# Attention stage rebuilt: token-major projections, head norms along rows, transposes on TensorE, output projection by chunks of its input

## The chip, the cores and the metric

The kernel runs on one core of one Trainium2 chip, as one program. The metric is the device time of one execution in microseconds. Three executions of the kernel before were timed, and one more was recorded by the hardware profiler.

## The reference, cut to what matters

The network is a trunk of two layers on 256 tokens of 1024 features, all in float32. Each layer is a gated feed-forward block (FFN), a mixer, a second FFN and a gated embedding. The mixer of layer 0 is the attention that this change rebuilds; layer 1's mixer is a pooling.

```python
x = x + 0.5 * swiglu(rms_norm(x, norm_ffn1[i]), w_ffn1_gu[i], w_ffn1_down[i])
h = rms_norm(x, norm_mix[i])
mix = stick_breaking_attention(h, w_qkv[j], q_norm[j], k_norm[j], w_o[j])   # layer 0
x = x + mix
x = x + 0.5 * swiglu(rms_norm(x, norm_ffn2[i]), w_ffn2_gu[i], w_ffn2_down[i])
gate = jax.nn.sigmoid(rms_norm(x, norm_ple[i]) @ w_ple_gate[i])
x = x + gate * (p[i] @ w_ple_proj[i])

def stick_breaking_attention(h, w_qkv, q_gain, k_gain, w_o):   # 16 heads of 64
    q, k, v = jnp.split(h @ w_qkv, 3, axis=-1)
    q = rms_norm(q.reshape(B, S, N_HEADS, HEAD_DIM), q_gain)   # a norm for each token and head
    k = rms_norm(k.reshape(B, S, N_HEADS, HEAD_DIM), k_gain)
    ...
    z = q @ k.T / 8                                            # for each head, causal
    log_stay = jnp.where(causal, jax.nn.log_sigmoid(-z), 0.0)
    log_after = lax.cumsum(log_stay, axis=3, reverse=True) - log_stay
    weights = jnp.where(causal, jnp.exp(jax.nn.log_sigmoid(z) + log_after), 0.0)
    return (weights @ v) @ w_o
```

The functions log_sigmoid and exp make ScalarE compute Abs, Exp and Ln for every score, and one more Exp for every weight.

## The kernel before, in words

**Numbers in two parts.** TensorE multiplies in fp32r. To keep float32 accuracy each operand is split into a high part (a copy rounded to fp32r) and a low part (the difference), and each product is three matmuls (`mm3`: high by high, high by low, low by high). Activations lie feature-major: 128 features on the partitions, 256 tokens along the row.

**Weights.** They stream in units of 1 MB (128 partitions by 2048 floats). `load` starts the DMA of a unit, `divide` makes its high part (line 171 on ScalarE, sometimes line 169 on VectorE) and its low part (line 173 on VectorE or GpSimd). The table `SPLIT` says for each unit into how many pieces it is cut, how many high parts VectorE makes, and how many low parts GpSimd makes. A unit not in the table is cut in two and split by ScalarE and VectorE. There are three buffers each of raw, high and low; `unit(u)` asks for the loads of units u to u+3 and for the split of u and u+1. Units 33 to 48 are the attention's, 49 is the embedding's projection, and the second FFN starts with unit 50.

**Order.** The order on TensorE and on the DMA queue is the order of the program text (`manual_schedule`). The order on ScalarE, VectorE and GpSimd is chosen by a list scheduler when the program is built; work inside `tc.high_priority()` goes ahead of other work, such as weight splits, as soon as it is ready. On the chip each engine executes its own list strictly in order.

**Attention before.** Heads are handled in eight pairs. For pair j, `heads_qk` multiplies the pair's q and k weights with the activations: 48 matmuls of 256 columns give q and k feature-major in one PSUM bank. `square_qk` squares it, twice on ScalarE, and splits the square; `norm_qk` sums the squares over the 64 features of a head by two 512-wide matmuls with a constant block matrix (`blkw`), then takes the root as Exp of -0.5 Ln, with a Newton step, on 128 by 512 elements, and writes the split q and k (lines 518 to 548). `scores` makes two score blocks (`late`: the last 128 keys by the last 128 queries, 256 wide for two heads; `all`: the first 128 keys by all queries, 512 wide), takes Abs, Exp and Ln of each (lines 566 to 568), and splits the result. `stick` adds the cumulative sums by matmuls with triangular constants, takes Exp, and splits the weights. `gather` multiplies them with the values v and splits the output `oh`, `ol`. The steps are ordered by two strings: `ITER` for one round of the loop over pairs 2 to 7 ("G Q0 N A S C Q1 X": gather of pair j-4, half of the projection, norm of pair j-1, stick of j-3, scores of j-2, the other half, squares), and `DRAIN` for the last pairs, in which pieces of the output projection (`W`) are mixed. Which of VectorE and GpSimd makes each copy and low part is set for every pair by letter tables (`SP_LOW`, `W_LOW`, `K_LOW`, `SQ_LOW` and others; "p" is GpSimd). The values are projected token-major between pairs 1 and 2. After the attention comes the layer's embedding projection (`embedding`, 48 matmuls), then the second FFN.

**Activation tables.** ScalarE holds one set of function tables at a time, and the build places an instruction ACT_TABLE_LOAD ahead of an activation whose function is not in the set that is loaded. `statistics`, the norm over all features, asks by hand for a set that holds both Ln and Exp (line 330, `preload_act_table_set`). The attention before begins with `statistics`. The pooling of layer 1 uses `token_scales` (lines 700 and 701: Ln, then Exp), which asks for no set.

Of the kernel before, what the change touches and what calls it, by code (L numbers as in the profile page):

```python
# [70 lines left out]
SP_HIGH = ("vv", "vv", "vv", "vv", "vv", "vv", "aa", "va")  # L71
SP_LOW = ("pv", "pp", "pp", "pp", "pp", "pp", "ps", "pv")
W_HIGH = ("vv", "vv", "vv", "vv", "vv", "vv", "vv", "av")
W_LOW = ("ps", "ps", "pv", "pv", "ps", "ps", "ps", "pv")

SQ_LOW = "vppvvvvv"
K_LOW = "pvvvppvv"

URGENT = ("exp", "o", "pw", "qk", "sp")

ITER = "G Q0 N A S C Q1 X"
DRAIN = (
    "W00 W03 G4 W02 N S5 C6 W01 W04 W10 W11 W12 W13 G5 "
    "S6 C7 W20 W21 G6 W14 W05 S7 W25 W06 W15 G7 W16 W23 W24"
)

@with_exitstack
def trunk(ctx: ExitStack, tc: tile.TileContext, gxT, pT, wts, outT):  # L90
# [13 lines left out]
    bufs_of = {"mm": 3, "z": 3, "st": 1, "o": 1}  # L104
# [12 lines left out]
    def next_bank():  # L117
        turn[0] += 1
        return bank("z" if turn[0] % 2 else "mm")
# [91 lines left out]
    blkw = const.tile([P, P], F32R, name="blkw")  # L211
    nc.gpsimd.memset(f(blkw), 0.0)
    for i in range(2):
        nc.gpsimd.memset(f(blkw[64 * i : 64 * i + 64, 64 * i : 64 * i + 64]), 1.0 / 64)
# [6 lines left out]
    ident = const.tile([P, P], F32R, name="ident")  # L221
    tri = const.tile([P, P], F32R, name="tri")
# [90 lines left out]
    def statistics(columns=False):  # L313
# [10 lines left out]
        if columns:  # L324
            for t in range(2):
                mm(st[:, S + t : S + t + 1], acc[:, t * P : (t + 1) * P], meanc, True, True)
# [8 lines left out]
        if not columns:  # L335
            return None
        ms = st[:, S : S + 2]
        rc = tmp.tile([P, 2], F32, tag="rc", bufs=1, name="rc")
        nc.scalar.activation(rc, ms, AF.Ln, bias=eps)
        nc.scalar.activation(rc, rc, AF.Exp, scale=-0.5)  # L340
        rsqrt_newton(rc, ms, EPS, 2, "rc")
        epsms = tmp.tile([P, S], F32, tag="epsms", bufs=1, name="epsms")
        nc.vector.tensor_scalar(
            out=epsms, in0=st[:, :S], scalar1=EPS, scalar2=EPS, op0=ALU.add, op1=ALU.mult
        )
        return rc, epsms

# [16 lines left out]
    def project_late(u, out, src, order, late):  # L364

        a, b = order[: NC - late], order[NC - late :]
        project(u, out, src, a, start=order[0], stop=order[-1])
        project(u, out, src, b, start=order[0], stop=order[-1])

    class Opening:  # L370
# [6 lines left out]
        def step(self, n=NC):  # L377
            for k in self.order[self.done :][:n]:
                for u, out in zip(self.us, self.banks):
                    project(u, out, self.src, (k,), start=self.order[0], stop=self.order[-1])  # L380
                self.done += 1

# [63 lines left out]
    def attention(u0, layer):  # L446
        uqk = [u0, u0 + 1] + [u0 + j for j in range(6, 12)]
        uv, uo = u0 + 2, u0 + 12
        with tc.tile_pool(name=name("attn"), bufs=1) as pool:
# [5 lines left out]
            gq = tmp.tile([P, 1], F32, tag="gq", bufs=1, name="gq")  # L455
            nc.vector.tensor_scalar_mul(gq, g[:, G_QK : G_QK + 1], 0.125)
            gk = g[:, G_QK + 1 : G_QK + 2]
# [8 lines left out]
            def urgent(what):  # L466
                return tc.high_priority() if what in URGENT else ExitStack()

            def copy(engine, out, v):
                if engine == "a":  # L470
                    nc.scalar.activation(out, v, AF.Copy)
                else:
                    nc.vector.tensor_copy(out, v)  # L473

            def low(engine, out, v, h, c):
                mid = (c.start + c.stop) // 2
                cuts = [c] if engine in "pv" else [slice(c.start, mid), slice(mid, c.stop)]
                for i, c in enumerate(cuts):
                    eng = nc.gpsimd if engine == "p" or engine == "s" and i else nc.vector
                    eng.tensor_sub(out[:, c], v[:, c], f(h[:, c]))  # L480

            sph, spl, wh_, wl_ = (
                pool.tile([P, S + 512], F32R, name=n) for n in ("sph", "spl", "pwh", "pwl")
            )
            qk, zs = {}, {}

            blocks = []
            for i in range(2):
                t = [pool.tile([P, 2, S], F32R, name=f"{n}{i}") for n in ("qh", "ql")]
                for v in t:  # L490
                    nc.gpsimd.memset(f(v[64:, 0]), 0.0)
                    nc.gpsimd.memset(f(v[:64, 1]), 0.0)
                blocks.append(t)

            def heads_qk(j, ps=None, halves=(0, 1)):
                ps = bank("mm") if ps is None else ps
                if j == 0:
                    project_late(uqk[j], ps, (xh, xl), list(range(NC)), 1)
                else:
                    project(uqk[j], ps, (xh, xl), halves=halves)  # L500
                return ps

            def square_qk(j, ps):
                sq = pool.tile([P, 512], F32, tag="qksq", name=name("qksq"))
                h = pool.tile([P, 512], F32R, tag="sqh", name=name("sqh"))
                lo = pool.tile([P, 512], F32R, tag="sql", name=name("sql"))
                with urgent("sq"):
                    nc.scalar.activation(h, ps, AF.Square)
                    nc.scalar.activation(sq, ps, AF.Square)
                    low(SQ_LOW[j], lo, sq, h, slice(0, 512))  # L510
                return h, lo

            def norm_qk(j, ps, sq):
                ms = bank("st")
                mm(ms, blkw, sq[0], True, False)
                mm(ms, blkw, sq[1], False, True)
                v = pool.tile([P, 512], F32, tag="qkv", name=name("qkv"))
                nc.vector.tensor_add(
                    v.rearrange("p (a b) -> p a b", a=2), ms.rearrange("p (a b) -> p a b", a=2),
                    dup(epsms),  # L520
                )
                y = pool.tile([P, 512], F32, tag="qky", name=name("qky"))
                nc.scalar.activation(y, v, AF.Ln)
                nc.scalar.activation(y, y, AF.Exp, scale=-0.5)
                t = pool.tile([P, 512], F32, tag="qkt", name=name("qkt"))
                nc.vector.tensor_mul(t, y, y)  # L526
                nc.vector.scalar_tensor_tensor(
                    out=t, in0=t, scalar=-0.5, in1=v, op0=ALU.mult, op1=ALU.mult
                )
                nc.vector.scalar_tensor_tensor(  # L530
                    out=y, in0=t, scalar=1.5, in1=y, op0=ALU.add, op1=ALU.mult
                )
                for i, gain in enumerate((gq, gk)):
                    c = slice(i * S, (i + 1) * S)
                    nc.vector.scalar_tensor_tensor(
                        out=y[:, c], in0=ps[:, c], scalar=gain, in1=y[:, c],
                        op0=ALU.mult, op1=ALU.mult,
                    )
# [3 lines left out]
                with urgent("qk"):  # L542
                    nc.scalar.activation(kh, y[:, S:], AF.Copy)
                    (nc.gpsimd if K_LOW[j] == "p" else nc.vector).tensor_sub(kl, y[:, S:], f(kh))  # L544
                    for a in range(2):
                        b = slice(64 * a, 64 * a + 64)
                        nc.scalar.activation(q[b, a], y[b, :S], AF.Copy)
                        nc.vector.tensor_sub(ql[b, a], y[b, :S], f(q[b, a]))  # L548
# [473 lines left out]
```

## Time and profile before

| | |
|---|---|
| three timed runs | 1023.67, 1023.89, 1026.84 us; median 1023.89 us |
| profiled execution | 1024.73 us, span 1023.0 us, mean granted TensorE clock 0.98 |
| TensorE (PE) busy | 982.4 us (96%) |
| VectorE (DVE) busy | 685.4 us (67%) |
| ScalarE (ACT) busy | 537.9 us (53%) |
| GpSimd (POOL) busy | 246.7 us (24%) |
| DMA | 174.79 MB, mean 171 GB/s |
| stage of attention and embedding | from 199.70 us to 361.83 us |

Times within the span are microseconds from its start. In the rows on waits, the engine ahead of the arrow waited for the one behind it. In rows grouped by line, "x18 | 17.0, 969" means 18 instructions, 17.0 us busy in all, 969 ns each in the mean. In the table by stretches each row has the stretch, its length, the busy time and the number of instructions of TensorE, its weight loads, VectorE, ScalarE and GpSimd, the granted clock, the busy share of the DMA engines and their GB/s.

### The profile page before, as it was taken

The numbers are of one execution on the slowest core, as the hardware profiler recorded it, in microseconds if no ns is written. First come the engines' busy times: TensorE is split into PE (matmuls) and PEld (weight loads), VectorE is DVE, ScalarE is ACT, GpSimd is POOL, SyncE is SP. The second block draws the span as 40 slices with busy tenths as digits, with TensorE's granted clock in tenths as the row PEclk, the third lists the DMA queues.
The fourth block names the chain that finished last, engine by engine and source line by source line (L and its number), as shares of the span: only waits on it lengthen the run. The fifth ranks groups of instructions, "written<-read, shape, count | busy, mean of one in ns | idle before, by whom it ended". The sixth has DMA issues, their size and how long they took to land.

```text
span 1023.0 us, 18925 instructions
## 1 busy us (share of the span) xinstructions
PE 982.4 (96%) x7888; PEld 963.3 (94%) x7888; DVE 685.4 (67%) x1022; ACT 537.9 (53%) x888; POOL 246.7 (24%) x293
## 2 busy tenths in 40 slices
PE   7999999998797899999999899999999999999997
PEld 7999999987687899999999899999998899999997
DVE  7956565578999857666556786565565785656574
ACT  5644444457677556454444664544346664444443
POOL 4300002865665531000051233000230200000262
PEclk9999999999898999999999899999999999999999
DMA  7655544544212246454544455555454355455531
GB/s 247 258 191 181 196 177 177 193 165 159 69 61 83 69 184 240 172 203 168 204 165 166 165 182 201 199 174 204 165 206 165 124 206 188 184 191 180 204 127 42
DMA packets 26294, 174.79 MB, mean 171 GB/s; under 512 B 2912, under 2 KB 3680, under 8 KB 5600
## 3 DMA queue, kind: packets, MB, share of 16 engines
q1 hardware_dynamic: 26208, 173.59, 47.0%
q8 instruction: 61, 1.00, 0.4%
q14 instruction: 25, 0.20, 0.1%
HBM read 172.53 MB, written 1.05 MB: 170 GB/s over the span
## 4 chain that ended last, share of the span: by engine, by line
PE 86%; DVE 10%; ACT 2%; issue 1%; DMA 0%; SPq 0%; DVEq 0%; ACTq 0%
PE mm L122 43%; PE z L122 42%; DVE wl L173 2%; DVE xx L289 2%; DVE ql L548 1%; PE o L122 1%; DVE sql L480 1%; DVE kl L544 1%; DMA gx<-gxT 0%; DVE sph L473 0%; DVE qkt L526 0%; DVE sp L570 0%; DVE ol L608 0%; DVE gx L866 0%; PE st L122 0%
## 5 line engine op out<-in xcount | busy, mean ns | idle before, releaser
L171 ACT ACTIVATE wh<-raw 128x1024 fp32r<-128x1024 f32 (+2 forms) x416 | 343.7, 857 | 312.9 <-PE z L122 126.2
L173 DVE TENSOR_TENSOR wl<-raw,wh 128x1024 fp32r<-128x1024 f32 (+2 forms) x342 | 360.5, 1072 | 105.9 <-ACT wh L171 104.9
L122 PE MATMUL mm<-xx,wh 128*128 128x256 f32 x1792 | 324.5, 282 | 0.0
L122 PE MATMUL z<-xx,wh 128*128 128x256 f32 x1536 | 277.9, 281 | 1.6 <-ACT wh L171 1.6
L122 PEld LDWEIGHTS mm<-xx,wh 128*128 128x128 f32 x1792 | 277.3, 190 | 0.5
L122 PE MATMUL mm<-xx,wl 128*128 128x256 f32 x896 | 252.4, 282 | 5.6 <-DVE wl L173 5.6
L122 PEld LDWEIGHTS z<-xx,wh 128*128 128x128 f32 x1536 | 236.7, 189 | 1.8 <-ACT wh L171 1.8
L122 PE MATMUL z<-xx,wl 128*128 128x256 f32 x768 | 216.0, 281 | 3.5 <-DVE wl L173 3.5
L122 PEld LDWEIGHTS mm<-xx,wl 128*128 128x128 f32 x896 | 170.3, 190 | 6.5 <-DVE wl L173 6.5
L122 PEld LDWEIGHTS z<-xx,wl 128*128 128x128 f32 x768 | 145.5, 190 | 4.2 <-DVE wl L173 4.1
L173 POOL TENSOR_TENSOR wl<-raw,wh 128x512 fp32r<-128x512 f32 (+1 forms) x83 | 128.0, 1561 | 84.8 <-ACT wh L171 71.6
L122 PE MATMUL z<-hx,wh 128*128 128x256 f32 x704 | 125.1, 280 | 0.0
L122 PE MATMUL mm<-hx,wh 128*128 128x256 f32 x704 | 125.1, 280 | 0.0
L293 POOL TENSOR_TENSOR acc<-gx 128x256 f32<-128x256 f32 x8 | 5.4, 670 | 486.0 <-DVE gx L441 425.3
L122 PEld LDWEIGHTS z<-hx,wh 128*128 128x128 f32 x704 | 107.5, 187 | 0.0
L122 PEld LDWEIGHTS mm<-hx,wh 128*128 128x128 f32 x704 | 107.5, 187 | 0.0
L122 PE MATMUL z<-hx,wl 128*128 128x256 f32 x352 | 98.2, 279 | 0.0
L122 PE MATMUL mm<-hx,wl 128*128 128x256 f32 x352 | 98.2, 279 | 0.0
L122 PEld LDWEIGHTS z<-hx,wl 128*128 128x128 f32 x352 | 66.1, 188 | 0.0
L122 PEld LDWEIGHTS mm<-hx,wl 128*128 128x128 f32 x352 | 66.1, 188 | 0.0
L288 ACT ACTIVATE xx<-gx 128x256 fp32r<-128x256 f32 x64 | 31.2, 504 | 66.3 <-DVE gx L441 52.7
L397 DVE TENSOR_TENSOR s<-mm,r 128x256 f32<-128x256 f32 x44 | 18.6, 422 | 57.3 <-PE mm L122 57.3
(221 smaller groups left out, 1072.0 us busy)
## 6 DMA issues: line engine op xcount, KB each, us to landing
raw<-wts SPq DMA_DIRECT2D x161, 1024.0 KB, 4.8
raw<-wts SPq DMA_DIRECT2D x7, 256.0 KB, 5.7
gx<-gxT SPq DMA_DIRECT2D x3, 256.0 KB, 5.5
outT<-gx SPq DMA_DIRECT2D x3, 256.0 KB, 2.6
p<-pT SPq DMA_DIRECT2D x2, 256.0 KB, 2.9
raw<-wts SPq DMA_DIRECT2D x2, 128.0 KB, 2.9
outT<-gx SPq DMA_DIRECT2D x2, 128.0 KB, 1.9
gx<-gxT SPq DMA_DIRECT2D x1, 165.0 KB, 2.4
```

Source lines behind the costliest of these rows:

```text
L122: nc.tensor.matmul(out, lhsT, rhs, start=start, stop=stop, skip_group_check=True)
L171: nc.scalar.activation(h[:, c], raw[u][:, c], AF.Copy)
L173: eng.tensor_sub(lo[:, c], raw[u][:, c], f(h[:, c]))
L288: nc.scalar.activation(xh[:, d], x[:, d], AF.Copy, scale=gc)
L289: nc.vector.scalar_tensor_tensor(out=xl[:, d], in0=x[:, d], scalar=gc, in1=f(xh[:, d]), op0=ALU.mult, op1=ALU.subtract)
L293: nc.gpsimd.tensor_mul(acc, x[:, d], x[:, d])
L397: nc.vector.tensor_mul(s, ps[:, :S], r)
L480: eng.tensor_sub(out[:, c], v[:, c], f(h[:, c]))
L544: (nc.gpsimd if K_LOW[j] == "p" else nc.vector).tensor_sub(kl, y[:, S:], f(kh))
L548: nc.vector.tensor_sub(ql[b, a], y[b, :S], f(q[b, a]))
```

## The change

- Q, k and v are all projected token-major (128 tokens on the partitions, 512 features along the row, that is 8 heads): six groups q0, k0, v0, q1, k1, v1, each of 8 steps of 6 matmuls of 512 columns. The weights are laid out accordingly.
- The norms of q and k are taken along rows for eight heads at once (`normalize`): a square on ScalarE, a row sum on VectorE, Ln, Exp and the Newton step on 128 by 16 elements, and a multiplication on VectorE. The matmuls with `blkw` go away.
- `transpose` turns q and k of a pair feature-major by four TensorE transposes of 128 by 128 into the one PSUM bank `st`; the gains and the scale 1/8 are applied to k in the copies.
- The order is one string, `HEADS`. The output projection `W` takes one 128-feature chunk of its input at a time and adds to all eight output tiles (four banks), so that they are all complete with W7; the residual additions follow. The embedding projection (`E`, on bank `st`) is moved ahead of the output projection.
- GpSimd makes no low parts there: units 33 to 55 are cut in four, high parts on ScalarE, low parts on VectorE, and the letter tables go away.
- The attention calls `token_scales` in place of `statistics`; the former sets no table. PSUM banks become 4 `mm` and 2 `z` (before 3 and 3).

```diff
-    32: (2, 0, 2), 34: (4, 0, 4), 35: (4, 0, 4), 36: (2, 0, 1), 37: (4, 1, 2), 38: (2, 0, 2),
-    41: (4, 0, 4), 42: (4, 0, 3), 43: (4, 0, 3), 44: (4, 0, 4), 45: (4, 0, 3), 46: (4, 0, 3),
+    32: (2, 0, 2), 33: (4, 0, 0), 34: (4, 0, 0), 35: (4, 0, 0), 36: (4, 0, 0), 37: (4, 0, 0),
+    38: (4, 0, 0), 39: (4, 0, 0), 40: (4, 0, 0), 41: (4, 0, 0), 42: (4, 0, 0), 43: (4, 0, 0),
...
-ITER = "G Q0 N A S C Q1 X"
-DRAIN = (...)
+HEADS = """
+q00 q01 q02 q03 q04 q05 N q06 q07 k00 k01 k02 k03 k04 k05 k06 k07
+v00 v01 v02 v03 T0 v04 v05 C0 v06 v07 q10 q11 S0 T1 q12 q13 C1 G0 q14 q15 q16 q17
+S1 T2 k10 k11 C2 G1 k12 k13 k14 k15 S2 T3 k16 k17 C3 G2 v10 v11 v12 v13 S3 T4 v14 v15 C4 G3
+v16 v17 E0 E1 S4 T5 W0 E2 C5 G4 E3 W1 S5 T6 W2 C6 G5 W3 W4 S6 T7 W5 C7 G6 W6 S7 G7 W7
+"""
-    bufs_of = {"mm": 3, "z": 3, "st": 1, "o": 1}
+    bufs_of = {"mm": 4, "z": 2, "st": 1, "o": 1}
+    def project_tokens(u0, ps, chunks):
+        for k in chunks:
+            wh, wl = unit(u0 + k // 4)
+            w = slice(k % 4 * 512, k % 4 * 512 + 512)
+            for t in range(2):
+                c = slice(t * P, (t + 1) * P)
+                mm(ps[t], xh[:, k, c], wh[:, w], k == 0, False)
+                mm(ps[t], xh[:, k, c], wl[:, w], False, False)
+                mm(ps[t], xl[:, k, c], wh[:, w], False, k == NC - 1)
+    def token_scales():
...
+        with tc.high_priority():
+            nc.scalar.activation(rc, st[:, :2], AF.Ln, bias=eps)
+            nc.scalar.activation(rc, rc, AF.Exp, scale=-0.5)
+            nc.vector.tensor_scalar(out=epsms, ...)
+            rsqrt_newton(rc, st[:, :2], EPS, 2, "rc")
+        return rc, epsms
+            def normalize(what, ps, epsms):
...
+                with tc.high_priority():
+                    for t in range(2):
+                        nc.scalar.activation(sq, ps[t]..., AF.Square)
+                        nc.vector.reduce_sum(out=ms[:, t], in_=sq, axis=mybir.AxisListType.X)
+                        nc.vector.tensor_scalar(out=ms[:, t], ...)
+                    nc.scalar.activation(r_, m, AF.Ln)
+                    nc.scalar.activation(r_, r_, AF.Exp, scale=-0.5)
+                    rsqrt_newton(r_, m, 0.0, 16, "rs")
+                    for t in range(2):
+                        nc.vector.tensor_mul(y[:, t]..., ps[t]..., rs[:, t]...)
+            def transpose(j):
+                st = bank("st")
+                for i, what in enumerate("qk"):
+                    for t in range(2):
+                        nc.tensor.transpose(st[:, o : o + P], normed[what, j // 4][:, t, c], identity)
...
+                    nc.scalar.activation(kh, st[:, S:], AF.Copy, scale=gk)
+                    nc.vector.scalar_tensor_tensor(out=kl, in0=st[:, S:], scalar=gk, in1=f(kh), ...)
                     for a in range(2):
+                        nc.scalar.activation(q[b, a], st[b, :S], AF.Copy)
+                        nc.vector.tensor_sub(ql[b, a], st[b, :S], f(q[b, a]))
             def scores(j):
...
+                    with tc.high_priority():
                         nc.scalar.activation(e, z, AF.Abs)
                         nc.scalar.activation(e, e, AF.Exp, scale=-1.0)
                         nc.scalar.activation(e, e, AF.Ln, bias=1.0)
...
+                        nc.vector.tensor_copy(sph[:, c], sp[:, c])
+                        nc.vector.tensor_sub(spl[:, c], sp[:, c], f(sph[:, c]))
+            def w_o(k):
+                wh, wl = unit(uo + k // 2)
+                if k == 0:
+                    ob.extend(bank("mm") for _ in range(4))
+                for m in range(NC):
+                    mm3(ob[m // 2]..., (wh[:, c], wl[:, c]), (oh[:, k], ol[:, k]), ...)
...
-            rc, epsms = statistics(columns=True)
+                elif what == "N":
+                    rc, epsms = token_scales()
```

More of the change, by code (lines that the diff above doesn't have):

```diff
@@ L210, in trunk @@
     nc.vector.memset(meanc, 1.0 / D)
[L211 to L214, printed above, removed]
     warm = bank("o")
@@ L311, in rsqrt_newton, with statistics @@
         nc.vector.tensor_mul(y, y, t)
-    def statistics(columns=False):
+    def statistics():
         nonlocal r
@@ L334, in statistics @@
             rsqrt_newton(r, st[:, :S], EPS, S, "r")
[L335 to L346, printed above, removed]
     def project(u, out, src, order=range(NC), halves=(0, 1), start=None, stop=None):
@@ L443, in ffn, with attention @@
         return u0 + UNITS_FFN
-    def attention(u0, layer):
-        uqk = [u0, u0 + 1] + [u0 + j for j in range(6, 12)]
-        uv, uo = u0 + 2, u0 + 12
+    def attention(u0, layer, embedding):
+        ue, uo = u0 + 12, u0 + 13
         with tc.tile_pool(name=name("attn"), bufs=1) as pool:
@@ L464, in pair @@
                 return t[:, c].rearrange("p (a b) -> p a b", b=n)
[L466 to L483, printed above, removed]
+            sph, spl, wh_, wl_, sp, w = (
+                pool.tile([P, S + 512], F32R if n[-1] in "hl" else F32, name=n)
+                for n in ("sph", "spl", "pwh", "pwl", "spv", "pwv")
             )
-            qk, zs = {}, {}
             blocks = []
@@ L503, in square_qk @@
[L503 to L538, printed above, removed]
@@ L539, in norm_qk @@
+            def transpose(j):
+                st = bank("st")
+                c = slice(j % 4 * P, j % 4 * P + P)
+                for i, what in enumerate("qk"):
+                    for t in range(2):
+                        o = (2 * i + t) * P
+                        nc.tensor.transpose(
+                            st[:, o : o + P], normed[what, j // 4][:, t, c], identity
+                        )
                 q, ql = blocks[j % 2]
@@ L563, in scores @@
                     zs[j].append((z, keys))
-                    e = pool.tile([P, 2, keys[1]], F32, tag=f"e{kt}", name=name("e"))
-                    with urgent("e"):
+                    e = pair(sp, keys)
+                    c = keys[0]
+                    with tc.high_priority():
                         nc.scalar.activation(e, z, AF.Abs)
@@ L568, in scores @@
                         nc.scalar.activation(e, e, AF.Ln, bias=1.0)
-                    with urgent("sp"):
                         nc.vector.scalar_tensor_tensor(
-                            out=pair(sp, keys), in0=z, scalar=0.0, in1=e, op0=ALU.max, op1=ALU.add
+                            out=e, in0=z, scalar=0.0, in1=e, op0=ALU.max, op1=ALU.add
                         )
-                        copy(SP_HIGH[j][1 - kt], sph[:, keys[0]], sp[:, keys[0]])
-                    with urgent("spl"):
-                        low(SP_LOW[j][1 - kt], spl, sp, sph, keys[0])
+                        nc.vector.tensor_copy(sph[:, c], sp[:, c])
+                        nc.vector.tensor_sub(spl[:, c], sp[:, c], f(sph[:, c]))
             def stick(j):
-                w = pool.tile([P, S + 512], F32, tag="w", name=name("w"))
                 (zl, _), (za, _) = zs[j]
@@ L638, in attention @@
-            ahead()
-            ps = ps1
-            for j in range(2, NPAIR):
-                nxt = bank("mm")
-                for step in ITER.split():
-                    if step[0] == "Q":
-                        heads_qk(j, nxt, (int(step[1]),))
-                    elif step == "G" and j >= 4:
-                        gather(j - 4)
-                    elif step == "S" and j >= 3:
-                        stick(j - 3)
-                    elif step == "N":
-                        norm_qk(j - 1, ps, sq)
-                    elif step == "C":
-                        scores(j - 2)
-                    elif step == "X":
-                        sq_next = square_qk(j, nxt)
-                    elif step == "A":
-                        ahead()
-                ps, sq = nxt, sq_next
@@ new lines, in attention @@
+            banks, rc, epsms = [], None, None
+            for step in HEADS.split():
+                what, n = step[0], step[1:]
+                if what in "qkv":
+                    group = "qkv".index(what) + 3 * int(n[0])
+                    k = int(n[1])
+                    if k == 0:
+                        banks = [bank("mm"), bank("mm")]
+                    project_tokens(u0 + 2 * group, banks, (k,))
+                    if k == NC - 1 and what == "v":
+                        c = slice(int(n[0]) * 512, int(n[0]) * 512 + 512)
+                        keep_tokens(vh[:, :, c], vl[:, :, c], banks, rc)
+                    elif k == NC - 1:
+                        normalize((what, int(n[0])), banks, epsms)
+                elif what == "N":
+                    rc, epsms = token_scales()
+                elif what == "E":
+                    embedding(int(n), tag="st")
@@ L675, in attention @@
                 else:
-                    {"G": gather, "S": stick, "C": scores}[step[0]](*n)
+                    {"T": transpose, "C": scores, "S": stick, "G": gather, "W": w_o}[what](int(n))
             begin_norm()
-            def residual(u, halves):
-                for d, ps in zip((2 * u, 2 * u + 1), halves):
-                    nc.vector.tensor_add(x[:, d], x[:, d], ps)
-                    norm_chunk(2, layer, d, d == 0, sqs=("mixer", 0))
-            for u in range(3):
-                w_o(u, *[k for k in range(NC) if k not in done[u]])
-                residual(u, (ob[u][:, :S], ob[u][:, S:]))
@@ L687, in attention @@
-            last = [bank("z"), bank("z")]
-            project(uo + 3, last, src)
-            residual(3, [t[:, :S] for t in last])
-        return u0 + 16
-    def token_scales():
-        st = bank("st")
-        for t in range(2):
-            mm(st[:, t : t + 1], acc[:, t * P : (t + 1) * P], meanc, True, True)
-        rc = tmp.tile([P, 2], F32, tag="rc", bufs=1, name=name("rc"))
-        with tc.high_priority():
-            nc.scalar.activation(rc, st[:, :2], AF.Ln, bias=eps)
-            nc.scalar.activation(rc, rc, AF.Exp, scale=-0.5)
-            rsqrt_newton(rc, st[:, :2], EPS, 2, "rc")
-        return rc
+            for d in range(NC):
+                with tc.high_priority():
+                    nc.vector.tensor_add(
+                        x[:, d], x[:, d], ob[d // 2][:, (d % 2) * S : (d % 2 + 1) * S]
+                    )
+                    norm_chunk(2, layer, d, d == 0, sqs=("mixer", 0))
@@ L712, in pooling @@
             parts = {}
-            def values(half, ps, chunks):
-                for k in chunks:
-                    wh, wl = unit(u0 + 2 * (1 - half) + k // 4)
-                    w = slice(k % 4 * 512, k % 4 * 512 + 512)
-                    for t in range(2):
-                        c = slice(t * P, (t + 1) * P)
-                        mm(ps[t], xh[:, k, c], wh[:, w], k == 0, False)
-                        mm(ps[t], xh[:, k, c], wl[:, w], False, False)
-                        mm(ps[t], xl[:, k, c], wh[:, w], False, k == NC - 1)
-            def keep(half, ps, rc):
-                c = slice(half * 512, half * 512 + 512)
-                with tc.high_priority():
-                    for t in range(2):
-                        nc.scalar.activation(uh[:, t, c], ps[t], AF.Copy, scale=rc[:, t : t + 1])
-                        nc.vector.scalar_tensor_tensor(
-                            out=ul[:, t, c], in0=ps[t], scalar=rc[:, t : t + 1],
-                            in1=f(uh[:, t, c]), op0=ALU.mult, op1=ALU.subtract,
-                        )
             def pool_window(gi):
@@ L969, in _weights @@
             w = a["w_qkv"][i // 2]
-            order = [t + half * NC for t in range(NC) for half in range(2)]
-            qk = _pairs(w[:, : 2 * D], order)
-            parts.append(qk[:2])
-            parts.append(w[:, 2 * D :].reshape(4, 2, P, D).transpose(0, 2, 1, 3).reshape(4, P, UNIT))
-            parts.append(qk[2:])
-            parts.append(_pairs(a["w_o"][i // 2]))
+            w = w.reshape(2, 4, P, 3, 2, 512).transpose(4, 3, 0, 2, 1, 5)
+            parts.append(w.reshape(12, P, UNIT))
             parts.append(_embed_unit(a["w_ple_proj"][i]))
+            w = a["w_o"][i // 2].reshape(4, 2, P, D)
+            parts.append(w.transpose(0, 2, 1, 3).reshape(4, P, UNIT))
         else:
```

170 lines of the change are left out of this document (70 added, 100 removed), and 16 rows, old and new, of the table SPLIT.

## The prediction

> **What bounds the kernel now.** I read the page's shares first, then the table by stretches, then who waited for whom.
>
> ```profile
> PE 982.4 (96%) x7888; PEld 963.3 (94%) x7888; DVE 685.4 (67%) x1022; ACT 537.9 (53%) x888; POOL 246.7 (24%) x293
> ```
>
> TensorE is the bound of the whole. The stretches show that it isn't in the stage that changes (the first row: from the first q matmul to the first of the second FFN):
>
> ```profile
> core 0: us, PE busy (x) PEld busy (x) DVE busy (x) ACT busy (x) POOL busy (x), PEclk, DMA share, GB/s
> 199.70:361.83 162.13, 140.75 (x906) 128.03 (x905) 140.07 (x209) 109.70 (x224) 98.15 (x89) 0.92 0.29 105
> 250.00:280.00 30.00, 23.68 (x145) 21.57 (x146) 28.98 (x46) 19.74 (x43) 19.01 (x16) 0.85 0.22 74
> 300.00:320.00 20.00, 12.46 (x77) 10.73 (x78) 19.74 (x26) 12.89 (x29) 16.17 (x14) 0.89 0.16 56
> 400.00:480.00 80.00, 80.00 (x681) 80.00 (x681) 48.40 (x71) 38.26 (x56) 0.00 (x0) 1.00 0.52 186
> ```
>
> In an FFN (last row) TensorE never rests: 681 matmuls of 256 columns in 80 us, 0.1175 us each. Among the pairs VectorE is full (28.98 of 30 us, 19.74 of 20) while TensorE rests and its granted clock falls to 0.85 and 0.89. The waits of TensorE in the stage name VectorE each time:
>
> ```profile
> PE z L122 <- DVE ql L548: 10.8, 5, 2.7
> PE st L122 <- DVE sql L480: 5.6, 3, 3.3
> PE z L122 <- DVE wl L173: 3.9, 2, 2.4
> PE z L122 <- DVE spl L480: 1.0, 2, 0.8
> ```
>
> That is 21.3 us. TensorE's need at full clock, in matmuls of 256 columns (one of 512 counts as two, as the pieces below show: 2.09/9 and 0.47/2, 0.233 us each): q and k 384, values 192, `blkw` 32, pairs 224, output 192, embedding 48, some for statistics: 126.5 us. So 162.1 - 126.5 = 35.6 us can be won at most: 21.3 of waits, 14.3 of lowered clock.
>
> ```profile
> 217.46 0.47 PE st L122 x2
> 217.93 2.09 PE z L122 x9
> ```
>
> VectorE is full partly because GpSimd works beside it. The same low part of a 128x512 weight piece takes 969 ns in the stage and 706 ns in a stretch of the pooling in which GpSimd makes none:
>
> ```profile
> L173 DVE TENSOR_TENSOR wl<-raw,wh 128x512 fp32r<-128x512 f32 x18 | 17.0, 969 | 0.2
> L548 DVE TENSOR_TENSOR ql<-qky,qh 64x256 fp32r<-64x256 f32 x16 | 15.4, 960 | 0.3
> ...
> L608 DVE TENSOR_TENSOR ol<-o,oh 64x256 fp32r<-64x256 f32 x16 | 6.7, 419 | 4.5 <-ACT oh L607 4.2
> ...
> L570 DVE SCALAR_TENSOR_TENSOR sp<-z,e 128x512 f32<-128x512 f32 x8 | 5.5, 684 | 0.3 <-ACT e L568 0.3
> ```
> ```profile
> L173 DVE TENSOR_TENSOR wl<-raw,wh 128x512 fp32r<-128x512 f32 x13 | 8.5, 706 | 6.3 <-ACT wh L171 6.3
> ```
>
> **The change part by part.** TensorE. The projections keep their columns: 0. `blkw` goes: -3.7 us. 32 transposes come; no row shows a plain float32 operand that is 128 wide, so each lies between a quarter of a 512-wide matmul (0.058 us, 1.9 in all) and a whole one (0.233, 7.5 in all). I take the upper end, nearer to an operand that isn't fp32r. Need after: 124.7 to 130.3 us.
>
> VectorE. It gets the low parts of GpSimd and loses the norm on 128x512. By the undisturbed rows, a copy taken no cheaper than 0.68 for 512 and 0.42 for 256: per pair, kl 0.42, ql 0.84, the maximum with zero 1.10, copies 2 x 1.10, low parts 2 x 1.13, ol 0.84: 7.7; eight pairs 61. Weights 68 pieces x 0.706 = 48. Norms: two sums and two products, estimated at the 0.68 of the 512-wide row, and six narrow ones, estimated at the 0.26 of ScalarE's narrow row below: 4.3, four groups 17. Values 4 x 0.71, residual 16 x 0.42, token scales 1.3: 11. Sum 137 us against 140 now. It stays near TensorE's need, no more.
>
> ScalarE is where I expect the time to go.
>
> ```profile
> L171 ACT ACTIVATE wh<-raw 128x512 fp32r<-128x512 f32 x51 | 29.4, 622 | 10.9 <-PE mm L122 7.4 <-issue 3.5
> ...
> L547 ACT ACTIVATE qh<-qky 64x256 fp32r<-64x256 f32 x16 | 6.6, 414 | 6.5 <-DVE qky L535 6.3
> L607 ACT ACTIVATE oh<-o 64x256 fp32r<-64x256 f32 x16 | 6.0, 375 | 6.2 <-DVE ol L608 3.0 <-PE o L122 3.0
> ...
> L330 ACT ACT_TABLE_LOAD x2 | 2.6, 1283 | 0.0
> ```
>
> Today the stage has two table loads, both asked for by `statistics`, and then Ln and Exp alternate without one. One pair's scores in order of time:
>
> ```profile
> 329.06 0.38 ACT L566 ACTIVATE e<-z 128x256 f32<-128x256 f32 x1
> 329.47 0.42 ACT L567 ACTIVATE e<-e 128x256 f32<-128x256 f32 x1
> 329.80 0.58 ACT L566 ACTIVATE e<-z 128x512 f32<-128x512 f32 x1
> 330.27 0.41 ACT L568 ACTIVATE e<-e 128x256 f32<-128x256 f32 x1
> 330.58 0.62 ACT L567 ACTIVATE e<-e 128x512 f32<-128x512 f32 x1
> 331.23 0.63 ACT L568 ACTIVATE e<-e 128x512 f32<-128x512 f32 x1
> ```
>
> They end at 331.86: 2.80 us. The order is Exp, Ln, Exp, Ln (L567, L568, L567, L568). The new attention never calls `statistics`, so nobody asks for the common set. What a kernel without the request gets stands in the pooling, where `token_scales` runs Ln and then Exp:
>
> ```profile
> 777.98 1.28 ACT L700 ACT_TABLE_LOAD   x1
> 779.28 0.26 ACT L700 ACTIVATE rc<-st,eps 128x2 f32<-128x2 f32 x1
> 779.44 0.62 ACT L171 ACTIVATE wh<-raw 128x512 fp32r<-128x512 f32 x1
> 780.08 1.28 ACT L701 ACT_TABLE_LOAD   x1
> 781.37 0.21 ACT L701 ACTIVATE rc<-rc 128x2 f32<-128x2 f32 x1
> ```
>
> Each of the two has its own load: the set brought in for Ln doesn't serve Exp. If that holds in the attention, every change between Exp and Ln costs 1.283 us: token scales 2, four norms 2 each, and per pair 4 (Exp, load, Ln, load, Exp, load, Ln, load, Exp of the weights): 42 loads, 53.9 us.
>
> Two statements of the Trainium skill bear on this place. Its page "ScalarE: Activation LUTs", section "Table sets: the hidden batching unit", says that Ln followed by Exp needs one load, since one set has both; rows L700 and L701 show two, so I don't go by it, and what it would give is the first rival. The same page, section "What ACT_TABLE_LOAD costs", adds a drain of about 1380 ns to each 1283 ns; by it 42 switches would cost 112 us, and the stage would be some 58 us longer than the sum below. The trace agrees with the 1283 and not with the drain (the load ends at 779.26 and Ln starts at 779.28), so I give that outcome no chance that shows in the numbers.
>
> ScalarE per pair: kh 0.42, q 2 x 0.414, scores 2.80, weights' Exp 0.38 + 0.58, oh 2 x 0.375: 5.8. A round between two `stick`s has six projection chunks, or as much of W, so 1.5 units, six pieces: 3.7. Without loads 9.5 a round; with four loads 14.6. TensorE needs in a round 8.4 of chunks and 3.3 of pair work, with transposes 11.9 to 12.6; VectorE 7.7 + 6 x 0.706 = 11.9. So ScalarE becomes the bound of the round.
>
> The stage in three pieces. Up to S0: 16 steps of 1.40 us are 22.4; the norm of k0 (two squares 1.2, sum 0.7, narrow steps 1.6, Ln and Exp 0.5, a load not hidden 1.3, product 1.4, say 6.5) ends at 28.9, shortly after v03 at 28.0; transposes, two steps, the first score block: 32.5; scores with three loads 6.7, the copies of v0 between them 1.2, VectorE 1.9, S0 itself 1.0: 43. From S0 to S7: seven rounds of 14.6 = 102, and in two of them the norms of q1 and k1 (squares 1.2, narrow 0.5, loads 2.6) 8.6: 111. From S7 on nothing covers: Exp with its load, copy and low part 3.6, G7 1.1, oh and ol 1.2, W7 24 matmuls 2.8, residual, xh and xl of chunk 0 1.3: 10. Sum 164 us against 162.1, so +1.9 us.
>
> Edits that I cost at nothing, with their cover. GpSimd's absence: already in the 706 ns. z with two banks: each is freed by the Exp of the weights, ahead of the next C. Bank `st` shared by T and E: E1 waits for E0's copy, 0.6 us, where ScalarE is the bound anyway. The four banks of W0 wait for v1's copies behind E0, E1, S4 and T5. The DMA moves the same 17 units, the embedding's ahead of the last four, with a share of 0.29. The residual on VectorE (0.84 a chunk) runs ahead of the FFN's 1.41 us per step; the split of unit 51 may queue behind it, as the embedding's weights do now (3.9 us of waits): equal. Without that cover the last two cost up to 4 us. Units 53 and 55 lie under VectorE's 31.6 idle us of 80.
>
> The profiled execution took 1024.73, 0.84 above the median of the three runs. 1023.89 + 1.9 gives 1025.8; I say 1025.
>
> **The rivals.** First, faster: the loads don't come. (a) One load serves Ln and Exp throughout. For it: after L330 the chain above runs with none. Against it: L700 and L701. (b) They come, but in about half the number, where both Exp go ahead of both Ln because ScalarE is late: two a pair, 20.5 us less. Against it: the order in the rows above. The rounds are then bound by TensorE and VectorE at some 12.6, with the norms 2 x 3 more; (a) 41 + 88 + 6 + 10 = 145, (b) 147 to 151. Time 1007 to 1013.
>
> Second, slower: the serial chain of a pair sets the round, not ScalarE's load. From S: transposes 0.5, two steps 2.8, first block 0.5, scores with three loads 6.7, maximum, copy and low part of the last block 2.1, S 1.0: 13.5. It decides from 14.6 on, that is when 1.1 us, two weight pieces of 0.62, get into it. With TensorE at a clock of 0.85 (its 4.8 us become 5.6), a norm in the middle and transposes at 0.94 it is 16 to 17: seven rounds more by 2 give 1039. For it: now, too, the waits sit on one late operand (ql, 10.8 us) and the clock falls with them.
>
> **How the numbers follow.** ScalarE as the bound: 0.55, with its own range 1017 to 1034 (a load fewer per pair is -10 us, uneven filling of rounds at 93% is +8). First rival 0.30 ((a) 0.12, (b) 0.18), second 0.15. About 3 us (0.3%) is what a measurement here can tell from no change. Of the 0.55, 0.13 is faster, 0.24 the same, 0.18 slower; with the rivals: faster 0.43, same 0.24, slower 0.33. The range takes in most of the first rival and of the second: 1005 to 1036.
>
> **What would show it.** Right: some 40 ACT_TABLE_LOADs on the lines of Exp and Ln in the stage, ScalarE above 90% busy between S0 and S7, TensorE waiting for `sph`/`spl` and `wl` behind it, no wait on ql or sql, low parts near 0.7 us, a stage of about 164 us. Wrong: few loads and a stage under 152 us; or many loads with ScalarE idle a fifth of a round, the chain being longer; or FFN stretches that differ from before.

## The result: 2.4% slower, and the profile after

The changed kernel took 1049.42 us (median of four runs, 1047.6 to 1051.49) against 1023.85 us: a ratio of 1.0243, 95% interval 1.0216 to 1.0271, some 25 us. The forecast was 1025, its range ended at 1036. The profiled execution took 1050.12 us.

The share line of the page, for the whole execution:

```profile
PE 995.5 (95%) x7710; PEld 962.5 (92%) x7710; DVE 669.9 (64%) x1090; ACT 569.3 (54%) x910; POOL 142.2 (14%) x209
```

GpSimd lost 105 us of work; VectorE took it over and is still busy 15 us less; ScalarE gained 31 us. The table by stretches, cut at the first q matmul, the end of the first `stick` (S0), the end of the last (S7) and the start of the second FFN, with 8.5 us of that FFN behind. The part ahead of the stage, in which the change alters next to nothing, differs from execution to execution (it ends at 199.70 in the kernel before, at 197.97 here and between 193.46 and 200.34 in the runs below), so each stage is taken from its own first q matmul:

```profile
core 0: us, PE busy (x) PEld busy (x) DVE busy (x) ACT busy (x) POOL busy (x), PEclk, DMA share, GB/s
197.97:381.51 183.54, 148.05 (x727) 121.33 (x725) 121.34 (x259) 141.90 (x246) 10.19 (x19) 0.90 0.28 102
197.97:244.61 46.64, 41.52 (x181) 32.47 (x180) 30.95 (x67) 36.75 (x60) 2.46 (x8) 0.99 0.42 152
244.61:365.99 121.38, 99.39 (x516) 83.28 (x515) 79.18 (x170) 97.88 (x171) 0.00 (x0) 0.89 0.26 92
365.99:381.51 15.52, 7.13 (x31) 5.59 (x31) 11.21 (x23) 7.26 (x16) 7.73 (x11) 0.75 0.08 33
381.51:390.00 8.49, 8.49 (x49) 8.49 (x50) 3.45 (x7) 1.70 (x2) 1.12 (x1) 0.65 0.32 124
```

The stage takes 183.5 us where it took 162.1. In the seven rounds between S0 and S7 no engine is full: ScalarE is busy 97.88 of 121.38 us (81%), VectorE 65%, and TensorE's clock is 0.89. The waits of TensorE in the stage, longest first, no longer name one engine:

```profile
PE z L114 <- DVE xx L278: 6.5, 1, 6.5
PE z L114 <- DVE sph L558: 4.9, 4, 2.9
PE mm L114 <- ACT oh L589: 4.4, 2, 3.1
PE st L114 <- ACT proj L738: 4.4, 1, 4.4
PE z L114 <- ACT qh L533: 3.4, 3, 1.5
PE st L519 <- DVE y L505: 3.3, 4, 1.6
PE z L114 <- DVE spl L559: 3.2, 5, 1.3
PE z L114 <- DVE spv L555: 3.0, 3, 1.7
```

`sph`, `spl` and `spv` are what comes out of Abs, Exp and Ln. Why they are late shows in one pair's scores on ScalarE in order of time, in which a line without operands is a table load:

```profile
300.45 0.38 ACT L552 ACTIVATE spv<-z 128x256 f32<-128x256 f32 x1 [2.22 <-PE z L114]
300.86 0.42 ACT L553 ACTIVATE spv<-spv 128x256 f32<-128x256 f32 x1
301.30 1.28 ACT L554 ACT_TABLE_LOAD   x1
302.59 0.42 ACT L554 ACTIVATE spv<-spv 128x256 f32<-128x256 f32 x1
302.92 0.58 ACT L552 ACTIVATE spv<-z 128x512 f32<-128x512 f32 x1
303.51 1.28 ACT L553 ACT_TABLE_LOAD   x1
304.81 0.63 ACT L553 ACTIVATE spv<-spv 128x512 f32<-128x512 f32 x1
305.35 0.36 ACT L589 ACTIVATE oh<-o 64x256 fp32r<-64x256 f32 x1
305.73 1.28 ACT L554 ACT_TABLE_LOAD   x1
307.02 0.63 ACT L554 ACTIVATE spv<-spv 128x512 f32<-128x512 f32 x1
```

The six activations took 2.80 us before; from 300.45 to 307.65 they take 7.2. And ScalarE had stood idle for 2.22 us just before. All loads of the stage, by line (Ln of the scores L554, Exp of the scores L553, Exp of the weights L572, the norms L501 and L502):

```profile
L554 ACT ACT_TABLE_LOAD x13 | 16.7, 1283 | 0.2
L572 ACT ACT_TABLE_LOAD x7 | 9.0, 1283 | 0.1
L553 ACT ACT_TABLE_LOAD x5 | 6.4, 1283 | 0.1
...
L502 ACT ACT_TABLE_LOAD x4 | 5.1, 1283 | 0.1
...
L501 ACT ACT_TABLE_LOAD x3 | 3.8, 1283 | 0.1
```

With the two of the token scales that is 34 loads, 43.6 us; the forecast was 42 loads, 53.9 us. The longest single wait has another cause. The chain of waits at the end of the stage (the pieces from the last additions of W7's result on):

```profile
374.24 1.47 DVE gx L626 x4
375.70 0.77 DVE xx L278 x2
376.47 0.41 issue
376.88 4.59 DVE xx L278 x6
381.51 1.44 PE z L114 x5
382.95 1.28 PE mm L114 x6
```

All eight outputs of W are complete at once, so VectorE makes the eight low parts (`xx`, L278) in one go, and TensorE, one matmul into the FFN, goes on only when the eighth is done. The trace doesn't number the chunks. In the built program the scheduler has put them in the order 3 4 5 6 7 2 1 0, while the FFN takes them from 0; the run e3_chunk_order below tests this.

### The profile page after: what moved, and what is told of

It is laid out like the page before. It is cut to its first block, busy times and chain, and to the rows that moved or that the text cites. A ratio compares the mean times of both kernels' runs of the same rounds, so it can differ in the third digit from the quotient of the medians.

```text
span 1048.4 us, 18501 instructions
## 1 busy us (share of the span) xinstructions
PE 995.5 (95%) x7710; PEld 962.5 (92%) x7710; DVE 669.9 (64%) x1090; ACT 569.3 (54%) x910; POOL 142.2 (14%) x209
## 3 DMA queue, kind: packets, MB, share of 16 engines
q1 hardware_dynamic: 26208, 173.59, 46.6%
## 4 chain that ended last, share of the span: by engine, by line
PE 85%; ACT 8%; DVE 5%; issue 1%; DMA 1%; SPq 0%; POOL 0%; POOLq 0%
PE mm L114 57%; PE z L114 27%; ACT wh L163 1%; ACT L554 1%; DVE wl L165 1%; DVE xx L278 1%; ACT spv L554 1%; PE st L114 1%; ACT spv L553 1%; ACT L553 1%; DMA gx<-gxT 1%; ACT spv L552 0%; DVE pwl L574 0%; ACT oh L589 0%; ACT L572 0%
## 5 line engine op out<-in xcount | busy, mean ns | idle before, releaser
L114 PE MATMUL z<-xx,wh 128*128 128x256 f32 x1056 | 193.0, 283 | 7.7 <-DVE xx L278 6.5
L114 PE MATMUL mm<-hx,wh 128*128 128x256 f32 x968 | 172.3, 281 | 0.0
L114 PEld LDWEIGHTS z<-xx,wh 128*128 128x128 f32 x1056 | 164.1, 191 | 8.4 <-DVE xx L278 6.7
L114 PE MATMUL z<-xx,wl 128*128 128x256 f32 x528 | 149.0, 282 | 1.6 <-DVE wl L165 1.6
L114 PEld LDWEIGHTS mm<-hx,wh 128*128 128x128 f32 x968 | 148.5, 188 | 0.0
L114 PEld LDWEIGHTS z<-xx,wl 128*128 128x128 f32 x528 | 100.5, 190 | 2.0 <-DVE wl L165 2.0
L114 PE MATMUL mm<-wh,xx 128*128 128x512 f32 x240 | 82.6, 411 | 0.0
L114 PE MATMUL z<-hx,wh 128*128 128x256 f32 x440 | 78.5, 281 | 0.0
L114 PEld LDWEIGHTS z<-hx,wh 128*128 128x128 f32 x440 | 67.5, 188 | 0.0
L165 POOL TENSOR_TENSOR wl<-raw,wh 128x512 fp32r<-128x512 f32 (+1 forms) x34 | 56.6, 1682 | 40.9 <-ACT wh L163 38.0
```

What stands on the lines that cost most here:

```text
L114: nc.tensor.matmul(out, lhsT, rhs, start=start, stop=stop, skip_group_check=True)
L165: eng.tensor_sub(lo[:, c], raw[u][:, c], f(h[:, c]))
```

## The experiments

Differences below are between ratios to the kernel before, times 1024 us, as each run was compared with that kernel on its own chip.

**The request for the common table set alone (e1_tables).**

```diff
-        nc.scalar.activation(xh[:, d], x[:, d], AF.Copy, scale=gc)
+        newest_act = nc.scalar.activation(xh[:, d], x[:, d], AF.Copy, scale=gc)
...
-            nc.scalar.activation(rc, st[:, :2], AF.Ln, bias=eps)
+            with tc.issue_after(newest_act.ins):
+                tables = nc.scalar.preload_act_table_set("natural_log_exp_and_others")
+            with tc.issue_after(tables.ins):
+                nc.scalar.activation(rc, st[:, :2], AF.Ln, bias=eps)
```

The first two lines stand in `norm_chunk`, the others in `token_scales`.

> The changed kernel with one edit: token_scales asks for the table set that holds both Ln and Exp, so 33 or 34 of the 49 table loads of the program go (43 us of ScalarE). Theory 1 (the loads stand in the chain of each pair, three between its first scores and the next stick, so each round of some 17 us is longer by 3 x 1.28): the stage of 182.8 us loses about 7 x 3.9 + 3 = 30 us, time about 1020 us, and ScalarE's share of the stage falls from 77% to about 64%. Rival (the rounds are long because of the serial handoffs between TensorE, ScalarE and VectorE and TensorE's lowered clock; the loads only fill gaps of ScalarE, which was idle 23% of the stage): not over 10 us less, 1039 us or more.

Measured: ratio 0.9916 (0.9893 to 0.9939), 1015.15 us, 33 us less than the changed kernel. With this one request the change is faster than the kernel before. Its stretches, whole stage, up to S0, S0 to S7, and the rest:

```profile
200.34:349.92 149.58, 133.81 (x728) 111.25 (x726) 121.26 (x259) 98.93 (x213) 10.24 (x19) 0.98 0.34 125
200.34:241.50 41.16, 40.44 (x183) 32.34 (x182) 31.23 (x69) 26.14 (x53) 2.45 (x8) 1.00 0.47 172
241.50:334.55 93.05, 86.28 (x516) 73.33 (x514) 78.95 (x170) 65.52 (x145) 0.00 (x0) 1.00 0.31 116
334.55:349.92 15.37, 7.09 (x32) 5.58 (x32) 11.08 (x23) 7.27 (x16) 7.79 (x11) 0.76 0.14 56
```

The seven rounds shrink from 121.4 to 93.1 us, 4.0 us each. In the changed kernel 24 loads start in them, 3.4 a round, 30.8 us of ScalarE, so each cost 1.2 us there. Up to S0 nine loads go and 5.5 us with them, 0.6 each. The end, which has no load, stays as it was, 15.4 against 15.5.

The two rows of the rounds also say in what the price was paid. Both have 516 matmuls. TensorE idled 22.0 us with the loads and 6.8 without; it was busy 99.39 us at a granted clock of 0.89 and 86.28 at 1.00. So of the 28.3 us some 15 were waits and some 13 slower matmuls. Without the loads TensorE is busy 93% of the rounds.

**The kernel before without its request (e2_before_no_request).** The preload in `statistics` is left out for the attention's call (`if not columns:` around it).

> The kernel before with one edit: the statistics call of the attention asks for no table set, so 49 more loads come (63 us of ScalarE). Theory 1: ScalarE needs 110 + 62 = 172 us in a stage of 162 us and the loads stand in the chain of the pairs: at least 25 us longer, 1049 to 1065 us. Rival (loads fill gaps): under 10 us longer, below 1034 us.

Measured: 1.0451 (1.0427 to 1.0475), 1069.46 us, 46 us more for 49 loads, 0.9 each. The old structure pays for the missing request too, above the forecast. Its first wait is TensorE's on the squares, `PE st <- ACT sqh`, 20.1 us, a wait that the kernel before doesn't have.

**The chunk order (e3_chunk_order).**

```diff
-            opening = opening or Opening(u0, (xh, xl), list(range(NC)))
+            first = [3, 4, 5, 6, 7, 2, 1, 0] if n == 1 else list(range(NC))
+            opening = opening or Opening(u0, (xh, xl), first)
```

> The changed kernel with one edit: the second FFN of layer 0 takes the chunks of its input in the order 3 4 5 6 7 2 1 0, in which VectorE makes their low parts, and not 0 to 7. Theory (TensorE waits 6.5 us at the start of this FFN since the low part of chunk 0 is made last of the eight): the wait shrinks to 1 us or less and the clock falls less after it: 6 to 8 us less, about 1042 us. Rival (the weights of the FFN's second unit, split late too, are the next to be waited for): under 2 us less, 1047 us or more.

Measured: 1.0168 (1.0144 to 1.0191), 1041.55 us, 8 us less. The same place in the chain, now with a single low part ahead of TensorE and matmuls at full pace from the second group on (0.71 us for six, where it was 1.28):

```profile
377.22 0.54 DVE xx L278
377.80 0.86 PE z L114 x5
378.66 0.71 PE mm L114 x6
```

**The embedding's copies at high priority (e4_embedding_copy).** `with tc.high_priority():` around the copy to `proj`.

> The changed kernel with one edit: the copies that empty bank st after the embedding's matmuls are made at high priority. Theory (the embedding's second part waited 4.4 us for the first one's copy, which stood behind the scores and weight copies on ScalarE): 3 to 5 us less, 1045 us. Rival (the chain of the pair, not the embedding, ends the round, and the copy now stands ahead of it): no change, or up to 3 us more.

Measured: 1.0252 (1.0235 to 1.027), 1049.82 us: no change, and TensorE's wait of 4.4 us for `proj` is still there. The edit didn't shorten the wait, so it tells nothing on what the wait costs. With the request (e1_tables) it is 0.9 us.

**Both edits (e5_tables_order).**

> The changed kernel with both edits, the request for the common table set and the order 3 4 5 6 7 2 1 0 of the FFN's chunks. Theory (the two costs lie one after the other): 34 and 8 us less than the changed kernel, 1007 us. Rival (with the loads gone another wait takes the place of the chunk order's): 1012 us or more.

Measured: 0.9831 (0.9795 to 0.9867), 1005.25 us, 42 us less than the changed kernel; 33 and 8 add up.

**Loads at other places (e8_loads_elsewhere).** Both edits, and a load behind the last copy of q (`tc.issue_after`) and one behind the last Ln of each pair.

> As the kernel with both edits, with two table loads a pair put back at places where ScalarE waits: one after the copies of q (ahead of the scores) and one after the last Ln (ahead of the weights' Exp), 16 in all, 20.5 us of ScalarE. Theory (what the loads cost is their place in the chain scores to stick, not ScalarE's time): 0 to 6 us more than without them. Rival (ScalarE's total is what counts, as the prediction had it): 16 us or more.

Measured: 0.9919 (0.9887 to 0.9951), 1013.73 us, 9 us more than e5_tables_order (4 to 14 by the two intervals). It lies between the two expectations: a load there costs some 0.56 us (0.25 to 0.9 by the interval), one of the changed kernel's 33/34 = 1.0. Place counts, but loads in the gaps aren't free either: waits for `y`, made by way of ScalarE in the norms, grow from 0.9 to 3.4 us, those for `qh` from 1.8 to 3.3.

**Two loads a pair (e9_two_loads_a_pair).** In `scores`, both Abs and both Exp are issued ahead of the first Ln; no request. 39 loads are left of the program's 49.

> The changed kernel, without the request, with both Exp of a pair's scores ahead of both Ln: 39 table loads in the program in place of 49. Theory (each load between scores and stick lengthens the round by its 1.28 us): 10 to 15 us less than the changed kernel, 1034 to 1039 us. Rival (ScalarE idles a fifth of the stage and absorbs them): under 4 us less.

Measured: 1.0124 (1.0094 to 1.0154), 1035.22 us, 12 us less than the changed kernel (8 to 16) for ten loads, 1.2 us each: about the length of a load, 1.28, though ScalarE idles a fifth of the changed kernel's rounds.

**GpSimd's low parts put back (e7_with_gpsimd).** Both edits, and `SPLIT` of the kernel before. Its counts were written for the old sequence of units, so this is GpSimd's work in its old places, not its best use.

> As the kernel with both edits, but with the table SPLIT of the kernel before, so that GpSimd makes the low parts of many pieces of units 34 to 55. Theory (GpSimd slows VectorE beside it: 969 against 685 ns for the low part of a weight piece, and is slow itself): 3 to 10 us more than without it, 1010 to 1017 us. Rival (VectorE, busy 121 of 151 us there, is relieved): 1 to 4 us less.

Measured: 1.0020 (0.9997 to 1.0043), 1024.04 us, 19 us more than e5_tables_order (15 to 24 by the two intervals), above both forecasts. The stage by engines, first with GpSimd, then e5_tables_order without; it is 16.7 us longer:

```profile
198.76:360.12 161.36, 139.97 (x727) 114.77 (x726) 117.19 (x210) 95.36 (x198) 59.68 (x50) 0.96 0.33 118
```
```profile
193.46:338.16 144.70, 133.83 (x727) 111.14 (x725) 116.43 (x252) 96.83 (x209) 6.59 (x15) 0.99 0.35 129
```

VectorE's operations in the same order (low parts of scores and weights, `spl`, `pwl`, with both inputs in SBUF; `ol`, with one input in PSUM):

```profile
L565 DVE TENSOR_TENSOR spl<-spv,sph 128x512 fp32r<-128x512 f32 x8 | 8.4, 1056 | 0.1
...
L580 DVE TENSOR_TENSOR pwl<-pwv,pwh 128x512 fp32r<-128x512 f32 x8 | 7.2, 903 | 0.0
...
L596 DVE TENSOR_TENSOR ol<-o,oh 64x256 fp32r<-64x256 f32 x16 | 6.8, 422 | 6.8 <-ACT oh L595 6.4
```
```profile
L596 DVE TENSOR_TENSOR ol<-o,oh 64x256 fp32r<-64x256 f32 x16 | 6.8, 423 | 3.3 <-ACT oh L595 3.0
...
L565 DVE TENSOR_TENSOR spl<-spv,sph 128x512 fp32r<-128x512 f32 x8 | 5.5, 686 | 0.1
L580 DVE TENSOR_TENSOR pwl<-pwv,pwh 128x512 fp32r<-128x512 f32 x8 | 5.5, 685 | 0.0
```

With GpSimd working, an operation on two SBUF inputs takes 1056 or 903 ns in the mean in place of 686; one that reads PSUM takes 422 either way. A copy with one SBUF input isn't always spared: the cast `sph` of 128x512 takes 684 ns in the mean in place of 423. The Trainium skill's page "GPSIMD Engine Reference", section "1. Specifications", says that GpSimd shares its SBUF interfaces with VectorE, in contention with VectorE instructions "in a 2-port perf mode or with two SBUF inputs"; the rows of the low parts agree. No run shows in which mode the cast ran.

The means hide that single pieces are hit and others not: the pieces of `pwl`, 0.41 to 0.69 us without GpSimd, take 0.42 to 1.75 with it. One of TensorE's long waits, traced back:

```profile
258.26 4.36 POOL L165 TENSOR_TENSOR wl<-raw,wh 128x512 fp32r<-128x512 f32 x3 [4.28 <-ACT wh L163]
258.34 3.15 DVE L580 TENSOR_TENSOR pwl<-pwv,pwh 128x256 fp32r<-128x256 f32 x2
261.86 0.38 ACT L539 ACTIVATE qh<-st 64x256 fp32r<-64x256 f32 x1 [2.39 <-DVE ql L540]
262.29 0.58 PE L114 MATMUL z<-qh,kh 128*128 128x256 f32 x1 [2.73 <-ACT qh L539]
```

While GpSimd makes three weight pieces, two pieces of `pwl` take 3.15 us, which without GpSimd are 1.1 (0.42 and 0.69). The low part of q stands behind them, ScalarE's next copy of q behind that, and TensorE waits. Its waits for `qh` are the longest of this run, 10.0 us in place of 1.8. The old `SPLIT` also cuts some units in two, so that VectorE has five pieces of 1.41 us; what that costs was not tested apart.

**The kernel before without GpSimd's low parts (e11_before_no_gpsimd).** Units 33 to 55 split as in the changed kernel, and `v` for every letter of `SP_LOW`, `W_LOW`, `SQ_LOW` and `K_LOW`.

> The kernel before with one edit: units 33 to 55 split as in the changed kernel, and all low parts of the attention on VectorE, none on GpSimd. Theory (in the old structure VectorE has no room: 140 us busy in a stage of 162, and 90 us of GpSimd's pieces come to it as about 60, while its own two-operand pieces get shorter by about a third, 35 us): between 5 us less and 15 us more. Rival (GpSimd's contention is the main cost in the old structure too, as between the two versions of the new one, 19 us): 10 us less or more than that.

Measured: 1.0068 (1.0041 to 1.0095), 7 us more. VectorE is busy 139.7 us in the stage, as before (140.07): faster pieces, but more of them. TensorE's wait for `sql`, the low part of the squares, grows from 5.6 to 18.7 us.

**Another end of the order string (e10_drain).** `W2 C6 G5 W3 S6 T7 W4 C7 G6 W5 S7 W6 G7 W7`, with both edits.

> As the kernel with both edits (request and chunk order), with the end of the order string changed so that W6 stands between the last stick and the last gather: W3 S6 T7 W4 C7 G6 W5 S7 W6 G7 W7. Theory (with short scores the last stick, gather and W7 wait on one another: 1.7 us for oh ahead of W6, about 2 us in G7): 2 to 4 us less, a ratio to the kernel before of 0.980 or less. Rival (S6 then comes earlier than its scores are ready, and the wait moves there): no change, 0.983.

Measured: 0.9814 (0.9786 to 0.9841), 1003.49 us. The 1.7 us wait ahead of W6 is gone, but the interval overlaps that of e5_tables_order: no gain that can be told. Its median is the lowest of all runs.

## Why the prediction was wrong

Its first cause was right and decided the sign: no request for the table set, so Ln and Exp each bring their own. Take the loads out and the result is 0.9916.

The step that failed is "So ScalarE becomes the bound of the round", at 14.6 us. It added the loads to ScalarE's sum and let the sum set the round. ScalarE's work came out at 97.88/7 = 14.0 us a round, the norms included, yet the rounds took 121.38/7 = 17.3 us with ScalarE at 81%. What the loads lengthen is the chain from scores to stick: 4.0 us a round come off with the request, 1.2 us for each load that goes, 1.2 us again for each load taken out by e9_two_loads_a_pair, and about half of that is the price where they stand elsewhere (e8_loads_elsewhere). Nearly half of the price is TensorE's lowered clock. That was the second rival, at 0.15 and 1039 us; its chain, 13.5 us plus what may "get into it", came out at 17.3, just above its upper case of 16 to 17. Other work on ScalarE (weight copies, norms, `oh` between the last Exp and Ln) stands in the chain too; how much of the rest falls to each was not separated.

Term by term (forecast, measured): S0 at 43, 46.6; rounds with norms 111, 121.4; end 10, 15.5; stage 164, 183.5. The end was mis-sized by "residual, xh and xl of chunk 0 1.3": the wait was 6.5 us, as chunk 0's low part came last. The words "runs ahead of the FFN's 1.41 us per step" assumed an order that only the built program shows. Behind the stage I had put nothing; there the FFN began with a clock of 0.65 (8.49 us, so 3.0 us lost). After the FFN's start the changed kernel takes 666.9 us (1048.4 - 381.51), the kernel before 661.2, e3_chunk_order 661.4; of these 5.7 us the clock explains 3.0, the rest stays open.

Smaller points. 34 loads came, not 42: in some pairs both Exp went ahead of both Ln, as rival (b) allowed, and one of the norms' loads fell away. VectorE was over-priced, 137 against 121.3: a copy of 512 takes 0.42, not 0.68. So were the transposes: at full clock four take 0.35 us (258.96 to 259.31), 0.09 each, nearer to the lower end of 0.058 than to the 0.233 taken; where the clock is down they take 0.7. The edit costed at nothing that was not nothing in the changed kernel is the bank `st` shared by T and E: 4.4 us of waits in place of 0.6.

The first rival, 1007 to 1013 us without the loads, was close to the price: 1015 with the request alone, 1005 with the order. Its rounds of some 12.6 us, bound by TensorE and VectorE, came out at 13.3 with TensorE busy 93% of them.

What the change itself is worth, without its two slips: 1.7% (e5_tables_order). Neither half brings that alone. The new structure with GpSimd is at 1.0020, the old one without GpSimd at 1.0068. The new structure takes so much off VectorE (117 against 140 us, both with GpSimd) that GpSimd can be left out, and leaving it out makes VectorE's two-input pieces of 512 a quarter to a third shorter in the mean. The norms along rows are likely the main part of that; no run has them alone.

## What to carry to other kernels

When a change moves an operation to another helper, list what the old helper did on the side: here one request for a table set, worth 33 us. A cost on an engine with idle time isn't covered by that idle time when it stands between two engines that wait for each other: price it by the chain of one round, not by the engine's sum, and count the clock that TensorE loses while it waits. Where several results become ready at once, read in the built program in which order the scheduler takes them, and consume them in that order.

## What the runs showed of the hardware

Two things I had not expected. With GpSimd's low parts the kernel is 19 us slower, in a structure in which VectorE without them is busy 116 of 145 us: low parts on two SBUF inputs take up to 54% longer in the mean (1056 against 686 ns), single ones up to 1.79 us (`spl`), and what stands behind them on VectorE is late. And waits cost TensorE more than their length: after the 6.5 us wait six matmuls took 1.28 us where six take 0.71 at full clock, and in the seven rounds the loads cost about as much in slower matmuls (13 us) as in waits (15 us). The Trainium skill's page "TensorE: Matmul & The Clock Gate", section "Part 1: The HAM clock gate (the "warmup" mystery)", has the clock halved after idling; the rows fit, 0.71/1.28 being 0.55.
